# A decoder layer on one core: second-stage activations leave by O and K buffers, gate-column parts and token scratch trade their buffers, ScalarE copies one block sum

## The chip, the core and the metric

One Trainium2 chip, of which the kernel uses one core. Five engines work side by side, each on its own list of instructions: TensorE (PE, matrix products, results in PSUM banks), VectorE (DVE), ScalarE (ACT), GpSimd (POOL, which here mostly issues DMAs) and SyncE (SP, which issues the weight loads). The metric is the device time of one execution in microseconds (us), the median of three runs.

## The reference

One layer of a decoder for 512 tokens of 1024 channels, in f32. `mod = silu(c) @ w_mod + b_mod` gives six vectors: shift, scale and gate for the mixers (`sh_m, sc_m, gt_m`) and for the feed-forward part (`sh_f, sc_f, gt_f`).

```python
h = rms_norm(x, g_mix_norm) * (1 + sc_m) + sh_m
proj = h @ w_in                    # two attentions' q, k, v, an indexer, two gates
...
merged = sigmoid(gate_a) * (o_a @ w_br_dsa) + sigmoid(gate_b) * (o_b @ w_br_moba)
x = x + gt_m * (merged @ w_out)
h = rms_norm(x, g_ffn_norm) * (1 + sc_f) + sh_f
g_ff, u_ff = split(h @ w_gate_up)          # 1024 -> 2 * 2816
x = x + gt_f * ((silu(g_ff) * u_ff) @ w_down)
```

`o_a` is causal attention over the keys that an indexer picks for each query, `o_b` causal attention over blocks of 256 keys. The change touches only the feed-forward part, the two gate vectors, and the scratch of the steps around them.

## The kernel before

Every f32 operand of a product is split into a high and a low part that TensorE takes (`wh` and `wl` for weights; ScalarE casts the high part, VectorE subtracts it from the f32 value to get the low part), and a product is three matmuls: high by high, low by high, high by low (`mm3`). A weight load lands in one of three `st` buffers (SP issues it), ScalarE writes `wh` (three buffers), VectorE writes `wl` (three buffers), and with that `st` is free for the next load.

The feed-forward part runs over 11 groups `gi` of 256 inner channels. Groups 0 to 3 and 10 take whole products, and groups 4 to 9 quarters of a block scheme that saves products by sums of blocks ("tokens" are the sums on the activations' side, made by `token_task` between groups 0 and 4). Each group's activations are combined by `combine(gi, a0, a1)`: first-stage blocks, which the down projection's first half uses, and second-stage blocks (`second`), which go out to DRAM (two stores of 384 KB on the POOL queue, by `pool_dma`, L1260) and come back 200 to 300 us later in O or K buffers. Before the change all second-stage blocks were split into the pair (h, l) that `staging(3)` takes **from the weights' own buffers** `wh` and `wl`. Such a buffer is free again when its store has landed, and the next weights' cast needs it.

`gtf_task` makes the rows `gt_f` (two halves of 512 columns): eight weighted rows of `w_mod` are summed by VectorE (`column_sums`, `cg<-st,cs`), the sum is split (`halves`, parts in `gu`), two matmuls with a matrix of ones spread it over all partitions (`pstr<-gu,oner`), and VectorE adds the bias (`cg<-pstr,sc`).

In the down projection `shared_sums` closes a block product. The last of them (M5) is a PSUM bank per token half to which two sums are added, so VectorE reads that bank twice; `share` then multiplies with `gtf` and adds to the output rows `V`.

The order of all instructions is made ahead of time by a planner in the kernel's code: tasks are generators that yield what they wait for (`room(tag)`, a tile, a name), `spawn` and `step` place their instructions between matmuls by a table of costs (`Clocks`), and `held_back` says how much later than planned a task may be placed. All operations are recorded in one helper, at line 111 of the profile, so that groups go by names: `out<-in`. Buffer counts: O 4, K 4, cg 2, sc 2, gu 2, s 3, st/wh/wl 3 each; PSUM `pstr` 2, `pss` 1, `pspv` 1, `psacc` 4.

Of the kernel before, what the change touches and what calls it, by code (L numbers as in the profile page):

```python
# [117 lines left out]
def layer(ctx, tc, x, vecs, w_mod, w_in, gvecs, w_br_dsa, w_br_moba, w_out, w_gate_up, w_down, cosh, sinh, cosi, sini, out):  # L118
# [859 lines left out]
                load(k0 + 2 * n)  # L978
        return held, sums

    def halves(sums):

        yield room("gu", 2)
        hi, lo = (t("gu", [P, 512], F32R) for _ in range(2))
        yield sums
        se.copy(hi, sums)
        yield hi
        ve.tensor_tensor(out=lo, in0=sums, in1=hi.bitcast(F32), op=ALU.subtract)
        return hi, lo
# [19 lines left out]
        landed[0] = max(ck.dma, ck.ready[sums.tensor.name][0]) + 9.0  # L1009
        done(tile)  # L1010

    def mod_rows(acc, col0, tag, bias_tag=None):

        r0 = 24 + col0 // P

        def load_bias(tile):
            nc.sync.dma_start(tile.rearrange("p (a d) -> p a d", d=P), vecs[r0:r0 + 4].partition_broadcast(P))
            arriving(tile, 512)

        if bias_tag:  # L1020
            yield room(bias_tag)
            load_bias(bias := t(bias_tag, [P, 512]))
        yield from column_sums(col0, tag, acc)
        parts = yield from halves(acc)
        if not bias_tag:
            load_bias(bias := acc)
        yield parts + (room("pstr"), bias, lambda: ck.ready[parts[1].tensor.name][0] + 1.0)
# [3 lines left out]
        ve.tensor_tensor(out=acc, in0=pg, in1=bias, op=ALU.add)  # L1031
        done(pg, *parts)
        if bias_tag:
            done(bias)

    gtm = []
    landed = [0.0]
# [220 lines left out]
    def pool_dma(dst, src, out_of=None):  # L1258
# [9 lines left out]
            ck.ready[name] = (landed, None)  # L1268
        ck.last[name] = (landed, None)

    STAGED = range(4, 9)
    first_acts = {}

    def staging(n):

        uid[0] += 1
        return [wp.tile([P, n, 256], F32R, name=f"w{q}_{uid[0]}", tag="w" + q) for q in "hl"]
# [22 lines left out]
    def combine(gi, a0, a1):  # L1300

        first, other = slice(0, 256), slice(256, 512)
        yield a0, a1, room("gu", 2)
        s13, s4 = t("gu", [P, 2, 256]), t("gu", [P, 256])
        ve.tensor_tensor(out=s13[:, 0], in0=a0[:, other], in1=a1[:, other], op=ALU.add)
        ve.tensor_tensor(out=s13[:, 1], in0=a0[:, first], in1=a0[:, other], op=ALU.subtract)
        ve.tensor_tensor(out=a0[:, other], in0=s13[:, 0], in1=a0[:, first], op=ALU.subtract)  # L1310
        ve.tensor_tensor(out=s4, in0=a1[:, first], in1=a0[:, other], op=ALU.subtract)
        staged = gi in STAGED
        if gi < 4:
            yield a0, s13, room("g", 4)
            tiles = [t("g", [P, 2, 256], F32R) for _ in range(4)]
            ha, la, hb, lb = tiles
        elif staged:
            yield a0, s13
            h, l = staging(4)
# [12 lines left out]
        if staged:  # L1332
            first_acts[gi] = dp.tile([P, 2, 4, 256], F32R, name=f"first{gi}")
            for n, q in enumerate((h, l)):
                pool_dma(first_acts[gi][:, n], q, out_of=q)
            ready.add(f"staged{gi}")
        else:
            pair_tiles[gi] = tiles
            pairs[gi] = first_blocks(ha, la, hb, lb)
            ready.add(f"pair{gi}")  # L1340
        yield s4, a1
        v1 = a1.rearrange("p (a d) -> p a d", a=2)
        h, l = staging(3)
        se.copy(h[:, 0:2], v1)
        se.copy(h[:, 2], s4)
        yield h
        ve.tensor_tensor(out=l[:, 0:2], in0=v1, in1=h[:, 0:2].bitcast(F32), op=ALU.subtract)
        ve.tensor_tensor(out=l[:, 2], in0=s4, in1=h[:, 2].bitcast(F32), op=ALU.subtract)
        done(a1, s4)
        second_acts[gi] = dp.tile([P, 2, 3, 256], F32R, name=f"second{gi}")  # L1350
        for n, q in enumerate((h, l)):
            pool_dma(second_acts[gi][:, n], q, out_of=q)
        ready.add(f"stored{gi}")

    def up_done(gi, half=None):
# [49 lines left out]
        return units  # L1405


    QUARTERS = range(4, 10)
    token_sums = {}

    def token_task():
# [4 lines left out]
        for a in range(2):  # L1416
# [9 lines left out]

            def difference(u, r, c, r2, c2):

                v = t("sc", [P, 2, 256])
                ve.tensor_tensor(out=u, in0=block(hb, r, c), in1=block(hb, r2, c2), op=ALU.subtract)  # L1430
                yield
                ve.tensor_tensor(out=v, in0=block(lb, r, c), in1=block(lb, r2, c2), op=ALU.subtract)
                yield
                ve.tensor_tensor(out=u, in0=u, in1=v, op=ALU.add)
                done(v)

            yield room("sc", 2)
            u = t("sc", [P, 2, 256])
# [4 lines left out]
            yield room("sc", 2)  # L1443
            u = t("sc", [P, 2, 256])
            yield from difference(u, 1, 1, 0, 1)
            yield u
            yield from part(3, u)
# [161 lines left out]
    def gtf_task():  # L1609
        yield "ffn0"  # L1610
        for half in range(2):
            yield room("cg")
            gtf.append(t("cg", [P, 512]))
            yield from mod_rows(gtf[half], 5 * D + half * 512, "st", "sc")
        ready.add("gtf")


# [51 lines left out]
    def split_first_half(loaded):  # L1669

        c, st, b = loaded
        yield st, b, earliest("sc", "s")
        t2 = t(soonest("sc", "s"), [P, 512])
# [73 lines left out]
    def shared_sums(n, tt, acc):  # L1747
# [9 lines left out]
            kept["U3", tt] = fresh()  # L1757
            ve.tensor_tensor(out=kept["U3", tt], in0=acc, in1=kept["U2", tt], op=ALU.add)
        else:
            c22, c12 = fresh(), fresh()  # L1760
            ve.tensor_tensor(out=c12, in0=acc, in1=kept["U2", tt], op=ALU.add)
            ve.tensor_tensor(out=c22, in0=acc, in1=kept["U3", tt], op=ALU.add)
            done(kept["U2", tt])
            spawn(share(tt, c12, c22, kept["U3", tt]), slack=3.0, rank=2, on=(DVE,))

    def share(tt, c12, c22, u3):
        yield "gtf"
# [23 lines left out]
    def down_units(c, second):  # L1791
# [36 lines left out]

        def part(w, rows):
            begin(w)  # L1830
            held_back[0] = 0.0 if second or c < last else 1.0
            for n, a, b, tags in rows:
                for tt in range(2):
                    acc = bank(n, tt, tags)
# [135 lines left out]
```

## Time and profile before

| what | value |
|---|---|
| time before, median of 3 runs | 775.88 us (775.51 to 779.34) |
| the profiled execution's own time | 778.61 us |
| its span | 776.8 us |
| TensorE busy | 761.9 us, 98% |
| VectorE busy | 603.7 us, 78% |
| ScalarE busy | 412.6 us, 53% |
| mean granted TensorE clock | 0.994 |

The profile was taken from one execution. In the page, each engine has its busy time and share of the span; the list of waits says for what an engine sat idle (`PE pstr <- DVE s` is TensorE, about to write a `pstr` bank, released by VectorE's work on a tile `s`). In a timeline the bracket `[idle before <-releaser]` stands on the first instruction after the idle time. PEclk is the granted clock: 1.00 is 2.4 GHz, 0.50 is 1.2 GHz.

### The profile page before, as it was taken

How to read it: one execution, taken by the hardware profiler on the slowest of the kernel's cores; microseconds unless marked ns; L12 is line 12 of the kernel's file. 1: busy time of each engine (PE TensorE's matmuls, PEld its weight loads, DVE VectorE, ACT ScalarE, POOL GpSimd, SP SyncE). 2: the span in 40 equal slices, each digit the busy share in tenths (PEclk: the TensorE clock that was granted, in tenths of full speed). 3: DMA queues.
4: the chain of work that ended last, by engine and by line, in shares of the span. 5: the costliest groups of instructions: out<-in, count | busy, mean ns of one | idle time of the engine just before them, and what ended most of it. 6: DMA issues, size and time to landing. Idle time of an engine off the chain costs nothing.

```text
span 776.8 us, 10981 instructions
## 1 busy us (share of the span) xinstructions
PE 761.9 (98%) x3884; PEld 641.6 (83%) x3884; DVE 603.7 (78%) x1183; ACT 412.6 (53%) x885; POOL 62.2 (8%) x91
## 2 busy tenths in 40 slices
PE   7999999999999999999999989899999999999998
PEld 6887888888788878888889967789999998888786
DVE  6974889989699786248768856878788854997797
ACT  6763786779776747634445422454444432554341
POOL 2000012001111000000000000000110120121100
PEclk9999999999999999999999999999999999999999
DMA  9976352531135364334530166454566689579982
GB/s 317 350 214 220 85 178 71 180 113 55 47 85 199 105 211 146 131 109 138 162 108 16 53 211 208 117 168 131 195 196 191 187 251 355 189 257 396 316 315 83
DMA packets 87921, 137.10 MB, mean 176 GB/s; under 512 B 9008, under 2 KB 49272, under 8 KB 87228
## 3 DMA queue, kind: packets, MB, share of 16 engines
q1 hardware_dynamic: 80076, 105.75, 42.7%
q0 software_dynamic: 7792, 30.67, 11.1%
q8 instruction: 30, 0.49, 0.3%
q14 instruction: 23, 0.19, 0.1%
HBM read 117.52 MB, written 18.88 MB: 176 GB/s over the span
## 4 chain that ended last, share of the span: by engine, by line
PE 60%; issue 17%; DVE 10%; DMA 7%; SPq 2%; ACT 2%; POOL 2%; POOLq 0%; DVEq 0%; ACTq 0%
PE psacc L111 43%; PE pstr L111 8%; PE pspv L111 5%; PE pss L111 5%; DMA st<-in_w_down_dram 3%; DVE wl L111 2%; DMA second<-wl 2%; DVE H L111 2%; DVE s L111 2%; DVE sc L111 1%; SPq L184 1%; POOL second L1260 1%; DMA K<-in_w_mod_dram 1%; DVE pT L111 1%; DMA second<-wh 1%
## 5 line engine op out<-in xcount | busy, mean ns | idle before, releaser
L111 DVE TENSOR_TENSOR wl<-st,wh 128x1024 fp32r<-128x1024 f32 (+1 forms) x98 | 113.7, 1160 | 59.1 <-ACT wh L111 38.2
L111 ACT CAST wh<-st 128x1024 fp32r<-128x1024 f32 (+1 forms) x98 | 97.5, 998 | 60.5 <-DMA second<-wh 23.4
L111 PE MATMUL psacc<-wh,H 128*128 128x512 f32 x384 | 126.4, 400 | 0.9 <-ACT H L111 0.9
L111 PE MATMUL psacc<-H,wh 128*128 128x512 f32 x384 | 125.6, 409 | 0.0
L111 PEld LDWEIGHTS psacc<-wh,H 128*128 128x128 f32 x384 | 72.0, 188 | 16.4 <-ACT H L111 1.4
L111 PEld LDWEIGHTS psacc<-H,wh 128*128 128x128 f32 x384 | 71.3, 192 | 15.4 <-issue 2.1
L111 PE MATMUL psacc<-H,wl 128*128 128x512 f32 x192 | 75.8, 395 | 0.0
L111 PE MATMUL psacc<-H,O 128*128 128x256 f32 (+1 forms) x459 | 71.2, 295 | 1.2 <-DVE g L111 1.2
L111 PE MATMUL psacc<-wl,H 128*128 128x512 f32 x192 | 71.0, 390 | 0.0
L111 PEld LDWEIGHTS psacc<-H,O 128*128 128x128 f32 x459 | 62.8, 191 | 4.0 <-DVE g L111 1.6
L111 POOL TENSOR_TENSOR m<-m,mhalf 128x4 f32<-128x4 f32 (+1 forms) x24 | 28.7, 1194 | 390.7 <-DVE m L111 345.4
L111 PEld LDWEIGHTS psacc<-H,wl 128*128 128x128 f32 x192 | 36.7, 191 | 8.2
L111 PE MATMUL psacc<-K,O 128*128 128x256 f32 x288 | 43.4, 283 | 0.0
L111 PEld LDWEIGHTS psacc<-wl,H 128*128 128x128 f32 x192 | 36.2, 188 | 6.8
L111 PE MATMUL pspv<-H,wh 128*128 128x512 f32 x128 | 39.9, 393 | 0.0
L111 PE MATMUL pss<-H,wh 128*128 128x512 f32 x128 | 39.5, 390 | 0.0
L111 PE MATMUL psacc<-O,wh 128*128 128x512 f32 x128 | 39.4, 389 | 0.0
L111 PEld LDWEIGHTS psacc<-K,O 128*128 128x128 f32 x288 | 38.4, 192 | 0.0
L111 ACT ACTIVATE s<-s,att 128x256 f32<-128x256 f32 (+3 forms) x64 | 34.2, 562 | 4.0 <-DVE att L111 3.8
L111 ACT CAST wh<-s 128x512 fp32r<-128x512 f32 x17 | 10.6, 621 | 37.1 <-DVE s L111 12.6
L111 ACT CAST O<-pT 128x512 fp32r<-128x512 f32 x24 | 14.7, 621 | 26.1 <-DVE pT L111 25.6
L111 PEld LDWEIGHTS pspv<-H,wh 128*128 128x128 f32 x128 | 24.2, 189 | 5.1
(329 smaller groups left out, 1637.9 us busy)
## 6 DMA issues: line engine op xcount, KB each, us to landing
st<-in_w_in_dram SPq DMA_DIRECT2D x36, 512.0 KB, 3.6
K<-in_w_mod_dram SPq DMA_DIRECT2D x12, 1024.0 KB, 6.5
st<-in_w_gate_up_dram SPq DMA_DIRECT2D x24, 512.0 KB, 3.7
st<-in_w_down_dram SPq DMA_DIRECT2D x22, 512.0 KB, 5.8
st<-in_w_gate_up_dram SPq DMA_DIRECT2D x40, 256.0 KB, 3.8
K<-in_w_mod_dram SPq DMA_DIRECT2D x16, 512.0 KB, 5.6
O<-second POOLq DMA_DIRECT2D x7, 768.0 KB, 7.4
second<-wh POOLq DMA_DIRECT2D x11, 384.0 KB, 4.5
```

Of the source, the lines that this page charges most:

```text
L111: inst = f(*args, **kw)
L184: last_dma[0] = nc.sync.dma_start(st[:, :, o:o + n], src.rearrange("(k p) n -> p k n", p=P))
L1260: nc.gpsimd.dma_start(dst, src)
```

## The change

1. `combine` puts the second-stage blocks of groups 0 to 2, 9 and 10 ("apart") in an O buffer, or in whichever of K and O is free first for groups 9 and 10. Groups 3 to 8 keep `staging(3)`.
2. `token_task` takes its scratch from `cg` instead of `sc`, and `gtf_task` keeps `gt_f` in `sc` instead of `cg` and its parts in `cg` instead of `gu`. It waits for the token sums first, because both use `cg`. The bias is loaded into the sum's own tile once it has been split, and the matmuls may be placed 2 us after the bias is planned to land.
3. `split_first_half` takes its scratch `t2` from `cg` or `s` instead of `sc` or `s`.
4. The M5 bank is copied to SBUF by ScalarE, and the two additions follow in `share`, from SBUF.
5. In the last chunk of the down projection's first half `held_back` is 2.5 instead of 1.0.

```diff
-    def halves(sums):
+    def halves(sums, tag="gu"):
...
+        yield from column_sums(col0, tag, acc)
+        if parts_tag == "cg":
+            yield "token_sums"
+        parts = yield from halves(acc, parts_tag)
+        nc.sync.dma_start(acc.rearrange("p (a d) -> p a d", d=P), vecs[r0:r0 + 4].partition_broadcast(P))
+        arriving(acc, 512)
+        yield parts + (room("pstr"), lambda: ck.ready[acc.tensor.name][0] + (2.0 if parts_tag == "cg" else 0.0))
...
-        yield s4, a1
+        apart = gi < QUARTERS[0] - 1 or gi >= QUARTERS[-1]
+        yield (s4, a1) + ((earliest("O") if gi < QUARTERS[0] else earliest("K", "O"),) if apart else ())
         v1 = a1.rearrange("p (a d) -> p a d", a=2)
-        h, l = staging(3)
+        if apart:
+            x = t("O" if gi < QUARTERS[0] else soonest("K", "O"), [P, 2, 3, 256], F32R)
+            (h, l), space = (x[:, 0], x[:, 1]), (x,)
+        else:
+            (h, l), space = staging(3)
...
+        done(*space)
...
-                v = t("sc", [P, 2, 256])
+                v = t("cg", [P, 2, 256])
...
-            yield room("cg")
-            gtf.append(t("cg", [P, 512]))
-            yield from mod_rows(gtf[half], 5 * D + half * 512, "st", "sc")
+            yield room("sc")
+            gtf.append(t("sc", [P, 512]))
+            yield from mod_rows(gtf[half], 5 * D + half * 512, "st", "cg")
...
-            c22, c12 = fresh(), fresh()
-            ve.tensor_tensor(out=c12, in0=acc, in1=kept["U2", tt], op=ALU.add)
-            ve.tensor_tensor(out=c22, in0=acc, in1=kept["U3", tt], op=ALU.add)
-            done(kept["U2", tt])
-            spawn(share(tt, c12, c22, kept["U3", tt]), slack=3.0, rank=2, on=(DVE,))
+            m5 = fresh()
+            se.copy(m5, acc)
+            spawn(share(tt, m5, kept["U2", tt], kept["U3", tt]), slack=3.0, rank=2, on=(DVE,))
...
-            held_back[0] = 0.0 if second or c < last else 1.0
+            held_back[0] = 0.0 if second or c < last else 2.5
```

How this stands in the engines' lists, at three places.

**ScalarE between the groups 0 and 1**, before. `s_4440` and `gu_4468` are the second-stage blocks of group 0, `wh<-st` are weight casts, `gu_4577` is the high part of the gate columns' first half:

```order
L111 CAST g_4480<-s_4425 128x512
L111 CAST g_4482<-gu_4467 128x512
L111 CAST wh_4486<-st_4356 128x1024
L111 CAST wh_4497<-s_4440 128x512
L111 CAST wh_4497<-gu_4468 128x256
L111 CAST wh_4545<-st_4506 128x1024
L111 CAST wh_4582<-st_4552 128x1024
L111 CAST gu_4577<-cg_4450 128x512
L111 ACTIVATE s_4599<-pss_4457 128x512
```

and now:

```order
L111 CAST wh_4480<-st_4356 128x1024
L111 CAST g_4490<-s_4425 128x512
L111 CAST g_4492<-gu_4466 128x512
L111 CAST O_4504<-s_4440 128x512
L111 CAST O_4504<-gu_4467 128x256
L111 CAST wh_4535<-st_4484 128x1024
L111 CAST K_4275<-cg_4507 128x512
L111 CAST K_4274<-cg_4507 128x512
L111 CAST wh_4587<-st_4545 128x1024
L111 ACTIVATE s_4604<-pss_4456 128x512
```

The second-stage blocks are in `O_4504`, the weight cast behind them takes a `wh` that only weights have used, one weight cast has moved ahead of the blocks, and the gate columns' cast has left this place for the token sums' parts (`K<-cg`).

**TensorE, the first pair of gate-column matmuls** (`oner`), before, in the last chunk of group 1:

```order
L111 MATMUL pstr_4458<-H_3944,wh_4545 128x512
L111 MATMUL pstr_4458<-H_3946,wh_4545 128x512
L111 MATMUL pstr_4458<-H_3944,wl_4546 128x512
L111 MATMUL pstr_4624<-gu_4577,oner 128x512
L111 MATMUL pstr_4624<-gu_4578,oner 128x512
L111 MATMUL pspv_4460<-H_3944,wh_4545 128x512
```

and now, in group 2 (48 matmuls further on in the list, row 1981 after row 1933):

```order
L111 MATMUL psacc_4640<-H_3943,wh_4625 128x512
L111 MATMUL psacc_4640<-H_3945,wh_4625 128x512
L111 MATMUL psacc_4640<-H_3943,wl_4626 128x512
L111 MATMUL pstr_4722<-cg_4631,oner 128x512
L111 MATMUL pstr_4722<-cg_4632,oner 128x512
L111 MATMUL psacc_4639<-H_3943,wh_4625 128x512
```

The second pair has moved from row 2007, in group 2, to row 2130, in group 3. Both `pstr` banks (`pstr_4822`, last written at row 2120, and `pstr_4821`, at row 2126) hold sums of that chunk until they are read, and the pair needs one of them:

```order
L111 MATMUL pstr_4821<-H_3944,wl_4899 128x512
L111 MATMUL pspv_4823<-H_3944,wh_4898 128x512
L111 MATMUL pspv_4823<-H_3946,wh_4898 128x512
L111 MATMUL pspv_4823<-H_3944,wl_4899 128x512
L111 MATMUL pstr_4999<-cg_4813,oner 128x512
L111 MATMUL pstr_4999<-cg_4814,oner 128x512
L111 MATMUL pspv_4823<-H_3944,wh_4898 128x512
```

VectorE's read of `pstr_4822` (`s_4979<-pstr_4822,s_4979`) stands behind the silu of the chunk on ScalarE and, on its own list, behind the splits of the next group's weights.

**VectorE at the M5 sums**, before. `psacc_6557` and `psacc_6561` are the banks that the next chunk takes first, `psacc_6565` and `psacc_6575` are M5:

```order
L111 TENSOR_TENSOR g_7039<-psacc_6557,g_7029 128x512
L111 TENSOR_TENSOR wl_1172_7009<-st_6958,wh_1172_7008 128x1024
L111 TENSOR_TENSOR wl_1172_7011<-gu_6960,wh_1172_7010 128x512
L111 TENSOR_TENSOR g_7046<-psacc_6561,g_7034 128x512
L111 TENSOR_TENSOR g_7052<-psacc_6565,g_7029 128x512
L111 TENSOR_TENSOR g_7051<-psacc_6565,g_7039 128x512
L111 TENSOR_TENSOR g_7059<-psacc_6575,g_7034 128x512
L111 TENSOR_TENSOR g_7058<-psacc_6575,g_7046 128x512
```

and now, with M5 in `psacc_6559` and `psacc_6569`, which ScalarE has copied to `g_7044` and `g_7049`:

```order
L111 TENSOR_TENSOR g_7032<-psacc_6551,g_7022 128x512
L111 TENSOR_TENSOR wl_1170_7002<-st_6951,wh_1170_7001 128x1024
L111 TENSOR_TENSOR wl_1170_7004<-gu_6953,wh_1170_7003 128x512
L111 TENSOR_TENSOR g_7039<-psacc_6555,g_7027 128x512
L111 TENSOR_TENSOR gu_7009<-st_7007,gu_7009 128x512
L111 TENSOR_TENSOR g_7022<-g_7044,g_7022 128x512
L111 TENSOR_TENSOR g_7027<-g_7049,g_7027 128x512
L111 TENSOR_TENSOR H_7055<-st_6975,H_7054 128x1024
```

The matmul that waited for the second free `psacc` bank waited for VectorE's read of it; now its bank is one that ScalarE frees. ScalarE's two copies stand right behind the copy of `pstr` that it had there already:

```order
L111 COPY g_6999<-pstr_6535 128x512
L111 CAST wh_1170_7001<-st_6951 128x1024
L111 CAST wh_1170_7003<-gu_6953 128x512
L111 COPY g_7016<-pstr_6539 128x512
L111 COPY g_7044<-psacc_6559 128x512
L111 COPY g_7049<-psacc_6569 128x512
L111 CAST H_7054<-st_6975 128x1024
```

The cast `H_7054` behind them moves back by two copies. TensorE has the same number of matmuls before and now, VectorE the same additions, and the POOL queue the same stores and reloads.

## Rows read from the trace of the kernel before

**Rows 1.** The page's busy times: engine, busy us, share of the span, instructions.
```profile
span 776.8 us, 10981 instructions
...
PE   761.9 (98%) x3884; PEld 641.6 (83%) x3884; DVE 603.7 (78%) x1183; ACT 412.6 (53%) x885; POOL 62.2 (8%) x91
```

**Rows 2.** The list of waits of TensorE over the whole span: who waited for whom, us in total, times, longest.
```profile
PE pstr L111 <- DVE s L111: 3.2, 1, 3.2
...
PE pstr L111 <- ACT gu L111: 2.0, 1, 2.0
PE psacc L111 <- DVE g L111: 1.2, 1, 1.2
```

**Rows 3.** The span in windows, TensorE alone: stretch in us, its length, PE busy (matmul groups), granted clock, share of the DMA engines, GB/s.
```profile
463.10:467.90 4.80, 1.61 (x7) 1.00 0.86 244
467.90:471.30 3.40, 3.40 (x10) 0.50 0.71 239
...
485.00:488.30 3.30, 1.05 (x4) 1.00 0.52 160
488.30:491.70 3.40, 3.40 (x9) 0.51 0.72 211
```

**Rows 4.** The timeline of TensorE around the two pairs of gate-column matmuls: start, duration, engine, operation, and the idle time before it with its releaser.
```profile
462.69 0.62 PE L111 MATMUL pstr<-H,wh 128*128 128x512 f32 x2
463.15 0.39 PE L111 MATMUL pstr<-H,wl 128*128 128x512 f32 x1
466.73 0.73 PE L111 MATMUL pstr<-gu,oner 128*128 128x512 f32 x2 [3.19 <-DVE s L111]
...
485.01 0.39 PE L111 MATMUL psacc<-H,wl 128*128 128x512 f32 x1
487.42 0.49 PE L111 MATMUL pstr<-gu,oner 128*128 128x512 f32 x1 [2.02 <-ACT gu L111]
488.15 0.64 PE L111 MATMUL pstr<-gu,oner 128*128 128x512 f32 x1 [0.23 <-DVE gu L111]
```

**Rows 5.** The timelines of SP, POOL, ACT and DVE from 447 to 468 us, the rows ahead of the first of the two idle times.
```profile
448.99 0.89 SPq L184 DMA_DIRECT2D st<-in_w_gate_up_dram  x2
...
459.60 3.90 SPq L184 DMA_DIRECT2D st<-in_w_gate_up_dram  x6
...
449.62 0.72 POOL L1260 DMA_DIRECT2D second<-wh  x1 [27.79 <-ACT wh L111]
450.87 0.54 POOL L1260 DMA_DIRECT2D second<-wl  x1 [0.54 <-DVE wl L111]
...
456.57 1.05 ACT L111 CAST wh<-st 128x1024 fp32r<-128x1024 f32 x1 [7.25 <-DMA second<-wh]
463.17 1.05 ACT L111 CAST wh<-st 128x1024 fp32r<-128x1024 f32 x1 [5.55 <-DMA st<-in_w_gate_up_dram]
...
458.35 1.22 DVE L111 TENSOR_TENSOR wl<-st,wh 128x1024 fp32r<-128x1024 f32 x1 [6.34 <-DMA second<-wl]
...
464.25 1.23 DVE L111 TENSOR_TENSOR wl<-st,wh 128x1024 fp32r<-128x1024 f32 x1 [1.65 <-ACT wh L111]
465.39 0.68 DVE L111 TENSOR_TENSOR gu<-cg,gu 128x512 fp32r<-128x512 f32 x1
465.99 0.68 DVE L111 TENSOR_TENSOR s<-pstr,s 128x512 f32<-128x512 f32 x1
```

**Rows 6.** The same timelines from 476 to 490 us, ahead of the second idle time.
```profile
476.97 0.53 POOL L1260 DMA_DIRECT2D second<-wh  x1 [25.56 <-ACT wh L111]
...
482.96 1.05 ACT L111 CAST wh<-st 128x1024 fp32r<-128x1024 f32 x1 [6.28 <-DMA second<-wh]
486.75 0.62 ACT L111 CAST gu<-cg 128x512 fp32r<-128x512 f32 x1 [2.74 <-DVE cg L111]
...
485.18 1.53 DVE L111 SCALAR_TENSOR_TENSOR cg<-st,cs,cg 128x512 f32<-128x512 f32 x2
```

**Rows 7.** The time to landing of the six stores into `second` between 440 and 520 us, and the median landing of the 256 KB weight loads between 430 and 510 us (count, KB each, us).
```profile
DMA to landing us min/median/max: 4.1/6.0/7.4
...
st<-in_w_gate_up_dram SPq DMA_DIRECT2D x18, 256.0 KB, 3.6
```

**Rows 8.** The last idle time, at the M5 sums: TensorE's and VectorE's timeline, ScalarE's copy of a `pstr` bank, and the window before it (PE, PEld, DVE, ACT, POOL busy, clock, DMA share, GB/s).
```profile
731.24 0.97 PE L111 MATMUL psacc<-H,O 128*128 128x512 f32 x3 [1.17 <-DVE g L111]
...
728.77 1.21 DVE L111 TENSOR_TENSOR wl<-st,wh 128x1024 fp32r<-128x1024 f32 x1
729.90 0.68 DVE L111 TENSOR_TENSOR wl<-gu,wh 128x512 fp32r<-128x512 f32 x1
730.50 3.07 DVE L111 TENSOR_TENSOR g<-psacc,g 128x512 f32<-128x512 f32 x5
...
723.55 0.59 ACT L111 COPY g<-pstr 128x512 f32<-128x512 f32 x1
...
708.00:712.00 4.00, 4.00 (x19) 3.31 (x18) 3.56 (x7) 2.19 (x4) 0.27 (x1) 1.00 1.07 410
```

**Rows 9.** VectorE's timeline at the mixers' gate rows, and the landing of their bias there.
```profile
298.08 0.69 DVE L111 TENSOR_TENSOR cg<-pstr,cg 128x512 f32<-128x512 f32 x1 [1.20 <-PE pstr L111]
...
cg<-in_vecs_dram SPq DMA_DIRECT2D x1, 256.0 KB, 4.6
```

**Rows 10.** The list of waits from 640 to 777 us: ScalarE, waiting for a store at the beginning of the down projection.
```profile
ACT wh L111 <- DMA second<-wh: 7.4, 1, 7.4
```

More of the change, by code (lines that the diff above doesn't have):

```diff
@@ L979, in column_sums @@
         return held, sums
-    def halves(sums):
-        yield room("gu", 2)
-        hi, lo = (t("gu", [P, 512], F32R) for _ in range(2))
+    def halves(sums, tag="gu"):
+        yield room(tag, 2)
+        hi, lo = (t(tag, [P, 512], F32R) for _ in range(2))
         yield sums
@@ L1010, in mod_columns, with mod_rows @@
         done(tile)
-    def mod_rows(acc, col0, tag, bias_tag=None):
+    def mod_rows(acc, col0, tag, parts_tag="gu"):
         r0 = 24 + col0 // P
[L1016 to L1022, printed above, removed]
-        yield from column_sums(col0, tag, acc)
[L1024 to L1027, printed above, removed]
+        yield from column_sums(col0, tag, acc)
+        if parts_tag == "cg":
[4 more added lines that the diff above has]
+        yield parts + (room("pstr"), lambda: ck.ready[acc.tensor.name][0] + (2.0 if parts_tag == "cg" else 0.0))
         pg = ps("tr")
@@ L1030, in mod_rows @@
             te.matmul(pg, oner.to_broadcast([P, P]), part, start=n == 0, stop=n == 1)
-        ve.tensor_tensor(out=acc, in0=pg, in1=bias, op=ALU.add)
+        ve.tensor_tensor(out=acc, in0=pg, in1=acc, op=ALU.add)
         done(pg, *parts)
-        if bias_tag:
-            done(bias)
     gtm = []
@@ L1269, in pool_dma @@
         ck.last[name] = (landed, None)
+    QUARTERS = range(4, 10)
     STAGED = range(4, 9)
@@ L1276, in staging @@
         uid[0] += 1
-        return [wp.tile([P, n, 256], F32R, name=f"w{q}_{uid[0]}", tag="w" + q) for q in "hl"]
+        return [wp.tile([P, n, 256], F32R, name=f"w{q}_{uid[0]}", tag="w" + q) for q in "hl"], ()
     def earliest(*tags):
@@ L1318, in combine @@
             yield a0, s13
-            h, l = staging(4)
+            (h, l), _ = staging(4)
             (ha, hb), (la, lb) = ((q[:, 0:2], q[:, 2:4]) for q in (h, l))
@@ L1405, in first_up @@
         return units
-    QUARTERS = range(4, 10)
     token_sums = {}
@@ L1435, in difference @@
                 done(v)
-            yield room("sc", 2)
-            u = t("sc", [P, 2, 256])
+            yield room("cg", 2)
+            u = t("cg", [P, 2, 256])
             yield from difference(u, 0, 1, 0, 0)
@@ L1442, in token_task @@
             done(u)
-            yield room("sc", 2)
-            u = t("sc", [P, 2, 256])
+            yield room("cg", 2)
+            u = t("cg", [P, 2, 256])
             yield from difference(u, 1, 1, 0, 1)
@@ L1671, in split_first_half @@
         c, st, b = loaded
-        yield st, b, earliest("sc", "s")
-        t2 = t(soonest("sc", "s"), [P, 512])
+        yield st, b, earliest("cg", "s")
+        t2 = t(soonest("cg", "s"), [P, 512])
         sums2[c] = dp.tile([P, 512], F32, name=f"sums{c}")
@@ L1759, in shared_sums, with share @@
         else:
-            c22, c12 = fresh(), fresh()
-            ve.tensor_tensor(out=c12, in0=acc, in1=kept["U2", tt], op=ALU.add)
-            ve.tensor_tensor(out=c22, in0=acc, in1=kept["U3", tt], op=ALU.add)
-            done(kept["U2", tt])
-            spawn(share(tt, c12, c22, kept["U3", tt]), slack=3.0, rank=2, on=(DVE,))
-    def share(tt, c12, c22, u3):
-        yield "gtf"
+            m5 = fresh()
+            se.copy(m5, acc)
+            spawn(share(tt, m5, kept["U2", tt], kept["U3", tt]), slack=3.0, rank=2, on=(DVE,))
+    def share(tt, m5, c12, u3):
+        yield "gtf", m5
+        ve.tensor_tensor(out=c12, in0=m5, in1=c12, op=ALU.add)
+        yield c12
+        ve.tensor_tensor(out=m5, in0=m5, in1=u3, op=ALU.add)
+        c22 = m5
         for i, half, c in ((2 + tt, 1, c22), (tt, 1, c12), (2 + tt, 0, u3)):
```

## The prediction

> **What bounds the kernel now.** I read the page's busy times first, then the list of what TensorE waited for, then the granted clock in windows around those waits, and last the timelines of the other engines ahead of each wait. TensorE is busy for 761.9 of 776.8 us and VectorE for 603.7 [rows 1], so TensorE is the bound, and only what leaves it idle or slow can be won. Past the kernel's start the list has three waits worth a change: 3.2 us for VectorE's work on `s`, 2.0 us for ScalarE's on `gu`, 1.2 us for VectorE's on `g` [rows 2]. The first two end at a pair of gate-column matmuls (`oner`), at 466.73 and 487.42 [rows 4], and behind each there are 3.40 us at half the clock, 0.50 and 0.51 [rows 3]. The clock fell after TensorE had stood idle there; after the third, shorter wait the windows show no such stretch.
>
> What the two cost: matmuls follow one another by 0.23 us at full clock (462.69 to 463.15 for two, [rows 4]).
> - First: 463.15 to 466.73 is 3.58, of which 0.23 is the matmul's own, so 3.35 lost; the half-clock stretch gives 3.40 x 0.50 = 1.70 less work. Together 5.05.
> - Second: 485.01 to 487.42 is 2.41, lost 2.18; 487.42 to 488.15 is 0.73, lost 0.50; the clock 3.40 x 0.49 = 1.67. Together 4.35.
> - Third: an idle of 1.17 [rows 8].
>
> Where do they come from? Followed back, the first [rows 5]: the pair needs a `pstr` bank, which VectorE frees with `s<-pstr` at 465.99; VectorE comes to it only behind `wl<-st` (464.25, waiting for ScalarE) and the gate columns' low part (465.39). ScalarE's cast at 463.17 waited 5.55 for a weight load, and SP issued these loads only from 459.60, since the `st` buffers came free with VectorE's `wl<-st` at 458.35. That one had waited 6.34, and ScalarE's cast at 456.57 had waited 7.25, both **for stores into `second` to land**, issued at 449.62 and 450.87. So the weights' pipe stands still for the landing of 384 KB that sit in the weights' own buffers. The second wait has the same head [rows 6]: store at 476.97, ScalarE's cast at 482.96 after 6.28 of waiting for it, then VectorE's column sums at 485.18, then the gate columns' high part at 486.75.
>
> **The change part by part.**
>
> *Second-stage blocks in O and K.* The casts and subtractions are the same, in number and size; the stores too. What goes is the wait of the weight casts for the store. The cast that ran at 456.57 then needs only its load. By the nearest row that load is issued at 448.99 and lands 3.6 us later [rows 5, 7], at 452.6, so the cast is 456.57 - 452.6 = 4.0 us earlier at least; the order has its `st` freed one cast sooner, which makes it more. The chain behind moves with it: loads at 459.60, cast at 463.17, bank read at 465.99. 4.0 is more than the 3.35 lost, so **by this part alone the first wait just goes**, with 0.6 to spare.
>
> *Gate columns.* The first pair stands 48 matmuls later in TensorE's list, 48 x 0.23 = 11 us, and the second 123 later. Their parts are ready long before: the sums that were complete at 465.39 are split when the token sums are done. I went through the lists of the engines from 440 to 512 us with the durations of the rows (cast 1.05, `wl` 1.22, half-size operation 0.68, load 3.6). By this the `wl` of each weight load between groups 1 and 3 is written 3.5 to 6 us before its first matmul, the first pair finds its parts 4 to 5 us early, and the second pair waits for the read of `pstr_4822`, which comes out 1.1 us early. So the second wait goes as well, and this last margin is the thinnest. With both, both half-clock stretches go: TensorE has no idle time left ahead of them. Gain 5.05 + 4.35 = **9.4 us**.
>
> *The other place of `mod_rows`.* The mixers' gate rows now load their bias after the split; VectorE's addition there, at 298.08, waited 1.20 for TensorE; the bias takes 4.6 to land [rows 9] and its issue is as early as before, but a small attention step of VectorE now stands behind that addition. Cost: between 0 and 0.5 us; I take 0.2.
>
> *M5.* Before, five additions at 730.50 stand behind `wl<-st` and `wl<-gu` (728.77, 729.90), and the bank that TensorE waits for is the first of them, free at 731.2 [rows 8]. Now that matmul takes a bank that ScalarE has copied; a copy of a bank is 0.59 [rows 8], ScalarE has finished two of them before 728, and TensorE comes to the bank at 730.1. So 1.17 goes, and with it the fraction of a matmul around it, 1.3 in all. What is late next: VectorE has the same work, less the banks, so the splits of the following weights are the next bound. In the same walk they come 0.3 to 0.8 us before their matmuls. ScalarE's cast behind the copies moves back by 2 x 0.59 = 1.2 and has that. Bounds of this part: 1.6 gained (with the small gaps beside it), or 0.3 lost if one of the tight splits is late by about its own margin again. I take 1.3.
>
> *Reloads.* With K and O used as staging at groups 9 and 10, the wait of 7.4 at the beginning of the down projection [rows 10] goes too; it cost TensorE nothing, so neither does its absence. Two of the reloads of `second` come 2 to 4 us later by the order of buffers, in a stretch in which the DMA engines are full (share 1.07 at 410 GB/s, [rows 8]). By the walk they are needed 25 us after that: 0. `held_back` and `t2` only moved instructions within the lists above and are counted there.
>
> Sum: 9.4 + 1.3 - 0.2 = 10.5 us. The profiled execution took 778.61 with a span of 776.8, so 1.8 lies outside the span and is not touched; its span would be 766.3. The median is 2.7 below the profiled execution. If those 2.7 are shorter waits for stores, the gain is 7.8 and not 10.5; I know no row that says so and take the whole, and keep 775.88 - 7.8 = 768.1 for the range. Forecast: 775.88 - 10.5 = **765.4**.
>
> **A rule that speaks against it.** The rows: the stores into `second` landed 4.1 to 7.4 us after their issue, median 6.0 [rows 7], and the cast at 456.57 was released by one. The Trainium skill, "DMA: Bandwidth & Descriptors", section "Anatomy of one DMA — SWDGE (gpsimd) path", gives a DMA that GpSimd issues 2.0 us plus its bytes at 436 GB/s, by my estimate 2.9 us for 384 KB. By that price the first store would be over at about 452.5, when the weights' load lands anyway, and taking the staging out of the way would bring nothing there. As a mechanism of this kernel, worked out from rows: if the weights' load and not the store held the cast, both long waits stay, only the third goes, and the time is 775.88 - 1.3 + 0.2 = 774.8. The trace differs from the page here: the store was slower than 2.9 us in each of the six, with the DMA engines busy at 0.52 to 0.86 in the windows around [rows 3], and ScalarE's wait ends with it.
>
> **The rivals.**
> - *One wait comes back at the moved pair.* The second pair stands ten matmuls behind the last one into `pstr_4822`, and its bank is read behind ScalarE's silu and VectorE's splits for the next group. Margin 1.1 us; one `wl` of 1.22 in front of that read uses it up. For: the same arrangement gave the first wait before. Against: in the list no such `wl` stands there. Price: that of the smaller old wait with its clock, 4.35. Time 765.4 + 4.4 = 769.8.
> - *The down projection gives nothing.* Splits with 0.3 to 0.8 us of margin in a stretch of full DMA: the wait at M5 moves to the next weights. Time 765.4 + 1.3 = 766.7, with another microsecond 767.7.
> - *The load, not the store, held the cast* (above): 774.8.
> - *Slower: O and K run short.* Each of the five groups keeps an O or K buffer until its store has landed, 6.0 us [rows 7]. If the next blocks that need such a buffer (the next group's weights, or the reload) had nothing to hide it, TensorE would wait 6.0 less what it has in hand, five times. At 4 us each that is 20, less the 10.5: 785. It decides against the change from 10.5 / 5 = 2.1 us a group on. Against it: the stores of two groups are issued 27 us apart (449.62 and 476.97, [rows 5, 6]), there are four O buffers, and by the walk the reloads lead by 25 us.
> - *The change doesn't do what it says:* the planner might give no O at the right time. The lists show `O<-s` for groups 0 to 2, so no chance is left for it.
>
> **How the numbers follow.** Forecast 0.62, one wait back 0.18, nothing in the down projection 0.10, load and not store 0.06, O and K short 0.04. A measurement of this kernel tells about 0.5% from no change, which is 3.9 us: below 772.0 is faster, above 779.8 slower. Faster are the first three, less some 0.03 for two of their prices at once: 0.87; the same 0.09; slower 0.04. Low end: 10.5 + 0.3 (M5's upper bound) + 0.2 (no cost at the gate rows), and some 0.9 for gaps too small for the list: 764.0. High end: the returned wait, with 0.5 for the gate rows and the tight splits: 770.3. That takes in the first three cases, and 768.1.
>
> **What would show it.** In the profile after: no wait of TensorE at either `pstr<-cg,oner` pair, no window below clock 1.00 between 440 and 520 us, no `ACT wh <- DMA second` there, and TensorE's list through group 3 some 9.4 us earlier, with the first mixers unchanged. At M5 no `psacc <- DVE g`. A wait of `pstr<-cg,oner` for `DVE s` with a half-clock stretch behind it is the first rival; a wait of ScalarE for `st` in its place is the third; waits of ScalarE or POOL for O or K with TensorE idle are the fourth. Wrong altogether would be the case in which the clock falls for another reason than the idle time before it.

## The result, and the profile after

The changed kernel takes 768.43 us (median of 4 runs, 767.38 to 769.08) against 776.04 before in the same session: ratio 0.9892, 95% interval 0.9861 to 0.9922, so it is faster by 6 to 11 us. The forecast was 765.4, its range 764.0 to 770.3. The profiled execution took 767.38, with a span of 765.6; before it was 778.61 and 776.8 [rows 1]. So the two profiled executions differ by 11.2 us, and the medians by 7.6. Most of this section is on the first number, and much of the experiments on the second.

The page's busy times after:

```profile
span 765.6 us, 10985 instructions
...
PE 756.6 (99%) x3884; PEld 639.2 (83%) x3884; DVE 603.6 (79%) x1183; ACT 413.1 (54%) x887; POOL 62.1 (8%) x91
```

The list of TensorE's waits after, with the same columns as [rows 2]:

```profile
PE pstr L111 <- DMA pT<-in_vecs_dram: 2.7, 1, 2.7
PE pstr L111 <- DMA K<-in_w_mod_dram: 1.1, 1, 1.1
PE psacc L111 <- ACT H L111: 0.9, 2, 0.7
PE pstr L111 <- DVE O L111: 0.7, 2, 0.4
```

None of the three waits of [rows 2] is left; what remains lies in the first 17 us. The windows that answer to [rows 3]:

```profile
463.10:467.90 4.80, 4.80 (x23) 1.00 0.58 187
467.90:471.30 3.40, 3.40 (x17) 1.00 0.74 201
...
485.00:488.30 3.30, 3.30 (x16) 1.00 0.86 261
488.30:491.70 3.40, 3.40 (x17) 1.00 0.67 190
```

TensorE is busy throughout, at the full clock. In each of the two windows of 3.40 us it starts 17 groups, where it had started 10 and 9. The timelines of POOL, SP, ACT and TensorE that answer to [rows 4 and 5]:

```profile
447.81 0.72 POOL L1253 DMA_DIRECT2D second<-O  x1 [25.92 <-ACT O L111]
...
447.25 0.88 SPq L184 DMA_DIRECT2D st<-in_w_gate_up_dram  x2
...
451.23 1.06 ACT L111 CAST wh<-st 128x1024 fp32r<-128x1024 f32 x1 [3.73 <-DMA st<-in_w_gate_up_dram]
...
474.32 0.63 PE L111 MATMUL pstr<-cg,oner 128*128 128x512 f32 x2
...
507.91 0.39 PE L111 MATMUL pspv<-H,wl 128*128 128x512 f32 x1
508.14 0.63 PE L111 MATMUL pstr<-cg,oner 128*128 128x512 f32 x2
```

The weight cast that stood at 456.57 behind the store now runs at 451.23, released by its load, while the store out of O is still under way (the two stores of this group landed 4.3 and 6.3 us after their issue). The load was issued at 447.25 instead of 448.99 [rows 5]. (In ScalarE's list ahead, the weight cast that has moved stood ahead of the blocks before, too; it is the two casts of `g` that it has passed.) Both pairs run without a gap, the second 0.23 us behind the matmul before it. At M5 (TensorE, ACT, DVE):

```profile
719.50 1.52 PE L111 MATMUL psacc<-H,O 128*128 128x512 f32 x6
...
716.30 1.27 ACT L111 COPY g<-psacc 128x512 f32<-128x512 f32 x2 [1.54 <-PE psacc L111]
...
717.73 0.68 DVE L111 TENSOR_TENSOR g<-psacc,g 128x512 f32<-128x512 f32 x1
```

The six matmuls into the two `psacc` banks follow one another; before, the second three waited 1.17 [rows 8].

The same can be read in a table of the times between matmuls of the same number (TensorE has the same list of 3884 in all of these kernels but for the moved pairs), taken from one profiled execution of each. The numbers count the profile's matmuls; a row of TensorE's list in the text ahead is its number less 393, so that the first pair stood at 2326 and stands at 2374, and the second stood at 2400 and stands at 2523. Number 2000 starts at about 413 us, ahead of group 0, and number 2500 stands in group 3. The last column ends with the start of the last matmul:

| kernel | its time, us | 2000 to 2500 | 2500 to 2800 | 2800 to end |
|---|---|---|---|---|
| before | 778.61 | 99.69 | 49.26 | 211.21 |
| before, once more | 776.00 | 97.06 | 49.26 | 210.67 |
| staging only | 769.65 | 91.67 | 49.26 | 210.13 |
| gate columns only | 775.08 | 90.24 | 56.13 | 210.12 |
| M5 only | 776.66 | 97.65 | 49.26 | 209.40 |
| M5 only, once more | 775.77 | 97.94 | 49.26 | 210.27 |
| staging and M5 | 768.26 | 90.85 | 49.26 | 209.40 |
| staging and gate columns | 767.43 | 90.24 | 49.29 | 209.40 |
| **changed** | 767.38 | 90.24 | 49.29 | 209.40 |
| before, stores twice | 782.86 | 100.73 | 49.26 | 212.72 |
| changed, stores twice | 766.81 | 90.24 | 49.28 | 209.40 |

The changed kernel's row has the smallest value of the first and the last column: 9.45 less than before up to 2500, 1.81 less from 2800 on. In the middle column nothing is gained (49.29 against 49.26).

### The profile page after: what moved, and what is told of

Same layout as the page of the kernel before. It is cut to its first block, busy times and chain, and to the rows that moved or that the text cites. A ratio compares the mean times of both kernels' runs of the same rounds, so it can differ in the third digit from the quotient of the medians.

```text
span 765.6 us, 10985 instructions
## 1 busy us (share of the span) xinstructions
PE 756.6 (99%) x3884; PEld 639.2 (83%) x3884; DVE 603.6 (79%) x1183; ACT 413.1 (54%) x887; POOL 62.1 (8%) x91
## 3 DMA queue, kind: packets, MB, share of 16 engines
q0 software_dynamic: 7792, 30.67, 11.2%
## 4 chain that ended last, share of the span: by engine, by line
PE 95%; SPq 2%; DVE 1%; DMA 1%; issue 0%; ACT 0%; ACTq 0%
PE psacc L111 62%; PE pstr L111 11%; PE pspv L111 11%; PE pss L111 11%; SPq L184 1%; DMA K<-in_w_mod_dram 1%; DVE V L111 1%; DVE s L111 1%; SPq L213 0%; SPq L222 0%; ACT gu L111 0%; ACT H L111 0%; SPq L206 0%; ACT acol L111 0%; ACT mcol L111 0%
## 5 line engine op out<-in xcount | busy, mean ns | idle before, releaser
L111 ACT CAST H<-st 128x512 fp32r<-128x512 f32 (+1 forms) x21 | 16.1, 766 | 27.5 <-PE psacc L111 26.9
L111 ACT CAST O<-pT 128x512 fp32r<-128x512 f32 x24 | 14.7, 621 | 25.2 <-DVE pT L111 24.7
```

The costliest lines, as they stand in the source:

```text
L111: inst = f(*args, **kw)
```

## The experiments

The times of each, with the ratio to runs of the kernel before on the same chip:

| run | median us (runs) | ratio, 95% interval |
|---|---|---|
| staging only | 769.31 (6) | 0.9898 [0.9870, 0.9927] |
| gate columns only | 776.08 (12) | 0.9984 [0.9964, 1.0005] |
| M5 only | 776.45 (12) | 1.0000 [0.9976, 1.0024] |
| before, once more | 776.91 (12) | 1.0014 [0.9992, 1.0036] |
| changed, once more | 768.07 (6) | 0.9892 [0.9872, 0.9912] |
| staging and gate columns, no M5 | 769.03 (6) | 0.9904 [0.9883, 0.9925] |
| before, stores twice | 779.99 (10) | 1.0037 [1.0013, 1.0061] |
| changed, stores twice | 768.08 (4) | 0.9908 [0.9878, 0.9938] |
| changed, more fill at start | 768.65 (5) | 0.9889 [0.9870, 0.9908] |
| changed, less fill at start | 768.49 (6) | 0.9898 [0.9873, 0.9923] |
| staging and M5 | 768.51 (6) | 0.9900 [0.9878, 0.9922] |
| M5 only, once more | 775.74 (12) | 0.9987 [0.9964, 1.0009] |

**1. The staging alone.** Theory: the stores hold the weights' buffers. Rival: the gate-column pair waits because of its place in the list.

```diff
+            x = t("O" if gi < QUARTERS[0] else soonest("K", "O"), [P, 2, 3, 256], F32R)
+            (h, l), space = (x[:, 0], x[:, 1]), (x,)
```

> The kernel before with the staging of the second-stage blocks in O and K buffers and nothing else; the instruction lists of TensorE and ScalarE keep their order, the gate-column pairs stay where they were. Theory (the stores hold the weight buffers, and that alone makes the two long waits): ScalarE's cast that waited 7.25 us runs about 4 us or more earlier, no wait of TensorE at either gate-column pair, the wait at M5 (about 1.2 us) stays; gain 6.0 us if the clock does not fall behind the waits in most runs of the kernel before, 9.4 us if it does. Rival (the pair's place in the list makes the wait): both waits stay, time within 2 us of before.

Measured: 769.31, 6.8 below before. ScalarE's cast and TensorE's two pairs, from the timelines:

```profile
453.84 1.05 ACT L111 CAST wh<-st 128x1024 fp32r<-128x1024 f32 x1 [5.54 <-DMA st<-in_w_gate_up_dram]
...
463.59 0.72 PE L111 MATMUL pstr<-gu,oner 128*128 128x512 f32 x2
...
480.27 0.39 PE L111 MATMUL psacc<-H,wl 128*128 128x512 f32 x1
481.18 0.49 PE L111 MATMUL pstr<-gu,oner 128*128 128x512 f32 x1 [0.53 <-ACT gu L111]
```

The cast waits for its load and no longer for the store, the first pair does not wait, the second is 0.91 behind its predecessor instead of 2.41 [rows 4], and no half-clock stretch is left in this execution. So the staging removes most of both waits while the pairs stay in place: the rival falls. Three expectations were missed. "No wait at either pair" is off by these 0.7 us at the second. The cast is 2.7 us earlier than at 456.57, not 4 or more, since the load is now what it waits for. And the wait at M5, which was to stay, is not in this profile's list.

**2. The gate columns alone.**

```diff
-            yield from mod_rows(gtf[half], 5 * D + half * 512, "st", "sc")
+            yield from mod_rows(gtf[half], 5 * D + half * 512, "st", "cg")
```

> The kernel before with the exchange of cg, sc and gu (token scratch, gate vectors, gate-column parts, the pairs 48 and 123 matmuls later) and nothing else; the second-stage blocks stay in the weight buffers. Theory: ScalarE still waits some 7 us for the store, and the weights behind it come 4 to 5 us later than with the staging moved, which uses up the 3.5 to 6 us that they are early there: TensorE waits 0 to 3 us at a weight, not at a pair; gain between 3 and 6 us. Rival (the pair's place makes the wait): no wait of TensorE of more than 0.5 us between 440 and 520 us, gain 6 to 9.4 us.

Measured: 776.08, no gain. ScalarE, TensorE and VectorE, from the timelines:

```profile
454.63 1.05 ACT L111 CAST wh<-st 128x1024 fp32r<-128x1024 f32 x1 [5.13 <-DMA second<-wh]
...
505.83 0.50 PE L111 MATMUL pss<-H,wl 128*128 128x512 f32 x1 [1.65 <-DVE wl L111]
513.64 1.22 PE L111 MATMUL pstr<-cg,oner 128*128 128x512 f32 x2 [3.22 <-DVE s L111]
...
511.70 1.29 DVE L111 TENSOR_TENSOR O<-pT,O 128x512 fp32r<-128x512 f32 x2
512.90 0.69 DVE L111 TENSOR_TENSOR s<-pstr,s 128x512 f32<-128x512 f32 x1
```

and the window of TensorE behind it (length, PE busy, clock, DMA share, GB/s):

```profile
513.20:516.70 3.50, 3.06 (x9) 0.51 0.39 133
```

This is the prediction's first rival, in a kernel whose staging is left as it was. The store still holds the weights: ScalarE waits 5.13 for the first, and behind the two others 6.50 and 6.51, where the profile names no releaser. Behind the third, TensorE first waits 1.65 at a weight, and then 3.22 at the moved second pair, whose bank VectorE reads behind the splits of the next group's weights (`O<-pT,O`); the half-clock stretch follows. Up to number 2500 the kernel is as fast as the changed one (90.24 in the table) and gives 6.87 back in the next column. My expectation had the wait at a weight and too small, 0 to 3; the rival's 6 to 9.4 us gained is refuted too. So the exchange of buffers pays only with the staging, where it takes off the last 0.6 to 1.4 us (91.67 and 90.85 to 90.24 in the table); the medians do not resolve that much.

**3. M5 alone.** The edit is that of `shared_sums` and `share` in the diff above, with `held_back`.

> The kernel before with M5 copied by ScalarE, the two additions from SBUF and the later placing in that chunk, and nothing else. Theory: the wait of TensorE for the psacc bank goes, gain 1.3 us (0.9 to 1.6), the two long waits stay. Rival (the splits behind are next, with no margin): a wait of about the same length at the next weights, gain 0 to 0.3 us.

Measured: ratio 1.0000. Yet the late column of the table is at its smallest, 209.40, and no wait for VectorE's `g` is in the list. Its 12 runs had low mean clocks, 7 of them 0.993 or less, so I ran it again at the end:

> The run with M5 alone, once more, because its traces and its times disagreed: its stretch from group 4 to the end was 1.3 us shorter than in the kernel before, its median no shorter, and 7 of its 12 runs had a mean clock of 0.993 or less, against 13 of 69 of the kernel before. Theory: the low clocks were chance; now the share of runs at 0.994 or less is that of before, about one in five, and the median is 0.8 to 1.8 us below before, with no wait in the late stretch. Rival: the edit brings half-clock stretches with it; again half of the runs or more at 0.994 or less, and the median equal to before within 0.5 us.

Now 2 of 12 were at 0.994 or less, so the low clocks did not come back in number. Over both, 9 of 24 runs had them, against 16 of 86 of the kernel before; whether the edit has a part in that is open. The median was 0.2 below before (interval -2.8 to +0.7), less than the 0.8 expected, and in this profile the late column is 210.27 with a wait of 0.4 for VectorE's `g`. In the late column, single executions have 211.21 and 210.67 without M5's copy and 210.27 and 209.40 with it. So M5 by itself is worth somewhere between nothing and 1.8 us, and the medians don't narrow it further.

**4. Before, once more.**

> The kernel before, unchanged, profiled again, for the clock. Theory on the 2.9 us by which the measured gain fell short: behind the two waits the clock falls in some executions only. Then the runs differ by steps of 1.7 us (one half-clock stretch of 3.4 us) around 776, 777.7 and 779.4, with mean clocks of 0.998, 0.996 and 0.994, and this profile shows the same two waits with fewer half-clock stretches behind them, or as many if its time is about 779. Rival (the waits themselves were longer in the first profile): the clock stretches are there in every run, and the two waits of 3.2 and 2.0 us differ by 1 us or more from one profile to the other.

Windows of TensorE in this execution, and its two waits at the pairs:

```profile
9.00:16.40 7.40, 6.66 (x48) 1.00 1.12 368
16.40:19.80 3.40, 3.40 (x10) 0.50 1.13 351
463.00:466.90 3.90, 1.12 (x5) 1.00 0.86 258
466.90:470.40 3.50, 3.40 (x8) 0.51 0.59 192
485.00:488.40 3.40, 1.84 (x7) 1.00 0.69 184
488.40:491.80 3.40, 3.40 (x17) 1.00 0.79 230
...
PE pstr L111 <- DVE s L111: 2.9, 1, 2.9
...
PE pstr L111 <- ACT gu L111: 1.3, 1, 1.3
```

Behind the first wait the clock falls as before, behind the second it doesn't (17 groups in 3.40 us), and another stretch stands at the kernel's start. The waits are shorter too: 2.9 and 1.3 against 3.2 and 2.0 [rows 2]. And the wait at M5 isn't there. Over 86 runs of the kernel before, the median is 776.4; 28 of them, with a mean clock of 0.998 or more, have a median of 775.4, and 16, at 0.994 or less, 780.0. So both theory and rival were partly right: clock stretches come and go, and the waits vary, though by less than the 1 us that the rival named.

**5. The changed kernel again, without M5, and with staging and M5.**

> The changed kernel, unchanged, profiled again. Theory: no wait of TensorE at the pairs or at M5 in this execution either, and the runs differ by 1.7 us, one half-clock stretch near the kernel's start (about 17 us), which the kernel before has as well in some runs; median 767.4 to 769.1. Rival: a run above 769 has its half-clock stretch or a wait at the moved pairs.

> The changed kernel with M5 added from the PSUM bank by VectorE as before (staging and gate columns changed, nothing else). Theory, after the run with M5 alone: with the two long waits gone VectorE is ahead at M5, so the copy gains nothing: within 0.5 us of the changed kernel, no wait for a psacc bank. Rival: the wait of 1.2 us at M5 is there, 1.3 us slower than the changed kernel.

> The changed kernel without the exchange of the gate columns' and tokens' buffers (staging and M5 only). Theory: the pairs stand where they were, and the second of them waits 0.5 to 1.0 us for its parts, as in the run with the staging alone, so the time is 0.5 to 1.5 us above the changed kernel and equal to the staging alone within 0.5. Rival (the exchange gains nothing by itself): equal to the changed kernel within 0.3 us, with no wait at the pairs.

The changed kernel: 766.5 to 767.4 at clock 1.00 and 768.8 to 769.6 at 0.998 or 0.999, no wait at the pairs or M5. Without M5: 0.6 to 1.0 above it by medians, within the noise, but its late column is also 209.40 and no `psacc` wait is in its list, so M5's copy is not needed once the other two are in. Staging and M5 without the exchange: 768.51, the pairs 0.6 us slower in the table (90.85), within the noise by the medians. That is less than the 0.5 to 1.5 us expected above the changed kernel, and it does not tell theory from rival.

**6. Stores twice.** In both kernels, for groups 0 to 2:

```diff
             pool_dma(second_acts[gi][:, n], q, out_of=q)
+            if gi < 3:
+                nc.gpsimd.dma_start(again[:, n], q)
```

> The kernel before, with each second-stage store of groups 0, 1 and 2 issued twice, the second time into DRAM that nobody reads; the lists of the other engines keep their order. Theory: the weight buffers are held until the second copy has landed, 3 to 6 us longer, so ScalarE's wait of 7 us grows to 10 to 13 and both waits of TensorE grow by about as much; time 6 to 14 us above before. Rival (the weights' load and not the store held the cast): within 1 us of before.

> The changed kernel with the same six stores issued twice. Theory: O buffers hold them and nobody needs these, so nothing waits: within 0.7 us of the changed kernel. Rival (O buffers are as short as the weights'): a wait at the next weights that take an O buffer, 2 us or more slower than the changed kernel.

In the kernel before, from ScalarE's timeline, TensorE's list of waits and its windows:

```profile
460.08 1.05 ACT L111 CAST wh<-st 128x1024 fp32r<-128x1024 f32 x1 [8.99 <-DMA again<-wh]
...
485.75 1.05 ACT L111 CAST wh<-st 128x1024 fp32r<-128x1024 f32 x1 [7.70 <-DMA again<-wh]
...
PE pstr L111 <- ACT gu L111: 3.4, 1, 3.4
PE pstr L111 <- DVE s L111: 3.3, 1, 3.3
...
PE pspv L111 <- DVE g L111: 1.3, 1, 1.3
...
469.70:473.10 3.40, 3.39 (x15) 1.00 0.67 201
...
491.90:495.30 3.40, 3.40 (x9) 0.50 0.70 221
```

ScalarE waits for the second copy, 8.99 and 7.70 instead of 7.25 and 6.28 [rows 5 and 6] (6.79 and 4.86 in the second profile of before), and the time rises by 2.9 us (interval 1.0 to 4.7). In the changed kernel the same stores cost nothing (768.08, against 768.07 and 768.43). So the cause is shown by doubling it. The sizes were well below what I expected. The second copy added 1.4 to 2.8 us to ScalarE's wait, not 3 to 6, since two stores land side by side (median 6.0 us after issue for the first copies, 7.0 for the second). TensorE's waits are 3.3 and 3.4 instead of 3.2 and 2.0, so only the second grew clearly. That all of the 2.9 us lies at these stores is not shown: in the profile the late column is 212.72 too, with a new wait of 1.3 us, and the only one of the ten runs at clock 1.00 took 774.38, below the median of before.

**7. The clock at the start.** Behind the second turn of tokens, four unused products more, and three more ahead of the first real ones; or, in the other direction, none and one.

```diff
-                unused_products(2)
+                unused_products(2 + 4 * i)
...
-        unused_products(3, xps[3])
+        unused_products(6, xps[3])
```

> The changed kernel with more of the products at the start whose results nobody uses: four more behind the second turn of tokens, where TensorE in some executions waits 1.1 us for the first rows of w_mod, and three more (six for three) ahead of the first real products, where it waits 0.67 us. Theory (the runs 1.7 us above the fastest have a half-clock stretch at about 17 us, behind this idle time): no run with clock 0.998, median 766.5 to 767.6. Rival (that stretch is elsewhere, or the clock falls for another reason): half of the runs at 0.998 as before, or the added products delay the start, median 768 to 770.

> The same in the other direction: the changed kernel without the unused products behind the first two turns and with one instead of three ahead of the first real products. Theory: the half-clock stretch near 17 us in all runs, clock 0.998 or below, median 769 to 771, and the profile shows it. Rival: no more 0.998 runs than without the edit, median 767 to 769.

With less fill, all six runs have 0.998 or less. TensorE's waits there:

```profile
PE pstr L111 <- DMA K<-in_w_mod_dram: 1.8, 1, 1.8
PE psacc L111 <- ACT H L111: 1.2, 2, 1.0
```

and its windows:

```profile
9.00:17.60 8.60, 5.74 (x44) 1.00 1.12 363
17.60:21.10 3.50, 3.50 (x10) 0.51 1.13 360
```

With more fill none of five runs is below 0.999. So the amount of unused work ahead of it changes how often the half-clock stretch at the start comes: in none of five, 4 of 10 and six of six runs, by the mean clock. The 1.7 us between the changed kernel's own runs fit one such stretch, but no run of it that had one was profiled. The idle time of a single execution does not decide it. The changed kernel's profile has no stretch at the start, behind this window:

```profile
9.00:16.40 7.40, 5.66 (x44) 1.00 1.12 356
```

The second profile of before (experiment 4) was busier in the same window, 6.66 us, and has one. The medians do not follow the clock at the start either: with more fill 768.65, where I had expected 766.5 to 767.6, and with less fill 768.49, where I had expected 769 to 771, against 768.43 and 768.07. With more fill the profile shows 0.5 us of the wait left, and seven matmuls more in the list. A version that beats the changed kernel did not come of it.

## Why the prediction was right, and where its size was off

*The cause.* The store of the second-stage blocks held the weights' buffers: shown by experiment 1 (undone, the waits go but for 0.7 us) and 6 (doubled, ScalarE's waits grow and the time rises; with the blocks elsewhere, neither). In the first profile the two stores of group 0 landed 6.9 and 7.4 us after their issue, at 456.5 and 458.3, and ScalarE's cast and VectorE's `wl<-st` follow at 456.57 and 458.35. The six landings before are 4.1 to 7.4 us [rows 7], the eight after 2.6 to 6.5 with a median of 5.0, and in both profiles of before ScalarE's cast was released by the store. By the rule of the Trainium skill, "DMA: Bandwidth & Descriptors", section "Anatomy of one DMA — SWDGE (gpsimd) path", such a store would be over in about 2.9 us (an estimate from its figures). The traces do not agree with it for these stores, and the rival built on it, 774.8, was not seen.

*The walk through the lists.* For the whole change it was right to a few tenths: the cast forecast for 452.6 or earlier ran at 451.23, the second pair without a wait, the list up to number 2500 9.45 us shorter where 9.4 was forecast. Against the profiled execution the whole sum was 10.5 and came out as 11.2; of the 0.7, 0.5 are small gaps from 2800 on (1.81 gained there, 1.3 forecast) and 0.2 the gate rows, which cost nothing. For the staging alone it was too good: the cast came 2.7 us earlier and not 4.0, so the first wait went with nothing to spare, and 0.7 us of the second stayed.

*The term that was mis-sized: the clock, with the waits of one execution.* 3.37 of the 9.4 us were the two half-clock stretches behind the waits, and I took the profiled execution's sum for the median. That execution, 2.2 us above the median of 86, had two stretches and the longer waits. The second one (776.00) is 2.63 us shorter up to number 2500: about 1.7 for the stretch behind the second wait that isn't there, and about 1.0 for waits of 2.9 and 1.3 instead of 3.2 and 2.0. And the changed kernel loses 1.7 us in some of its own runs (4 of 10 at clock 0.998), which I had not counted since the profile of before showed no stretch at the start. What the clock gives the medians can only be bounded. Of the runs with a mean clock of 0.999 or more, the kernel before has a median of 775.5 (9 of 86) and the changed one 767.4 (6 of 10), 8.1 apart, as far as those of all runs are (776.4 and 768.3); by this cut the clock brings nothing. A straight line through the 86 runs has 774.4 at clock 1.00, 2.0 below the median, where the changed kernel's runs at 1.00 are 1.0 below theirs; by it the clock brings about 1 us (both are estimates from the runs' times and clocks). Without the two stretches the sum is 9.4 - 3.37 + 1.3 - 0.2 = 7.1; measured were 7.6 by the medians of the session, 8.4 by the ratio. The prediction set aside that the 2.7 us above the median might be something that the median doesn't have, and kept 768.1 for the range only; that value was the right one, though in the second execution more of the difference was clock than shorter waits. That the measured time lies within the range is in part luck: its upper part was made for a wait that comes back, and none did.

*M5.* The mechanism is right (ScalarE frees the bank, no wait is left), its price is not one of the typical execution: in the second profile of before there is no such wait. VectorE's row behind the late weight load stands 3.1 us earlier there (723.26 against 726.36), TensorE's matmuls into the two banks only 2.0 (727.22 against 729.21), and 0.36 us is lost in the six of them (1.88 against 1.52 in the changed kernel). The late stretch does get shorter, by 1.3 to 1.8, but the staging and the exchange together do that without M5 (209.40). Why they do is not shown.

*The mixers' gate rows.* Forecast 0 to 0.5: the stretch of the list around them is equal within 0.1 us in the two profiles, so 0.

*The rivals.* The wait at the moved pair is real, 3.22 us with its clock stretch, but only where the staging is not moved. ScalarE does wait for `st` where it had waited for the store (14.7 us between 430 and 520, 6.1 before), which the prediction had named as the sign of the third rival; the sign was badly chosen, since TensorE waits for nothing there. O and K did not run short. Not settled is how much M5 is worth alone, and why the clock sometimes falls and sometimes not behind nearly equal waits (it did behind 1.6 us in one execution, that of M5 once more, and did not behind 3.3 in experiment 6).

## What to carry to other kernels

A buffer that is lent to an outgoing transfer is lost until the transfer has landed; if it belongs to the pipe that feeds the bottleneck, the whole pipe stops for the landing, and the wait shows up far away, at whatever stands behind that pipe in two other engines' lists. Follow the releasers back through the engines before pricing an edit, and try the parts singly: here one of three edits does nearly everything, and another, by itself, moves the wait on instead of removing it. Before a profile's sum is taken for the median, see how far that execution lies from the median, and price what varies between executions (clock stretches, landings in a full stretch) at less than full.

## What the runs showed of the hardware

- Half-clock stretches of 3.4 us (granted clock 0.50 to 0.51, 1.2 instead of 2.4 GHz; 8 to 10 matmul groups started instead of 17, so about 1.7 us each) come in some executions only: behind idle times of 3.2 and 2.0 us in one execution of the kernel before, behind the first but not behind the second (2.9, 1.3) in another, and with the stores doubled behind the second but not behind the first (3.3, 3.4). At the start, more unused work ahead of it left no run of five with a mean clock of 0.998 or less, and less work left it in six of six.
- Stores of 384 KB issued one right behind the other overlap: the second copies landed a median of 7.0 us after their issue, the first 6.0. With each store issued twice, ScalarE's waits for landing were 9.0 and 7.7 us, against 7.3 and 6.3, and 6.8 and 4.9, in two executions with single stores.
- The same kernel's waits for a landing differ from execution to execution: 6.3 and 4.9 us for ScalarE at the second store, and 2.0 and 1.3 for TensorE behind it. A wait of 1.2 us elsewhere was there in one of these two executions and not in the other.
